# Spreading the conditioning vector on TensorE and summing the squares of x there as they land, in a transformer block on Trainium2

## Chip, cores and metric

One Trainium2 chip, one of its cores. The metric is the device time of one execution of the program, in microseconds (us), the median of several runs. Inputs come from the chip's HBM and outputs go back to it. The engines are TensorE (PE, its weight loads are PEld), VectorE (DVE), ScalarE (ACT), GpSimd (POOL) and SyncE (SP); SPq and ACTq are the instruction queues of an engine where they issue DMAs or wait.

## The reference

A block of three sublayers on x of 512 tokens by 1024 channels, in float32: a feed-forward layer, a hybrid mixer (pooling and a chunked state-space scan), and a second feed-forward layer, then a last normalisation. Each sublayer is modulated by a conditioning vector c of 1024 numbers:

```python
mod = (silu(c) @ w_ada + b_ada).reshape(1, 3, 3, 1024)
shift, scale, gate = mod[:, :, 0], mod[:, :, 1], mod[:, :, 2]
h = rmsnorm(x, norm_g[0]) * (1 + scale[:, 0]) + shift[:, 0]
x = x + 0.5 * gate[:, 0] * swiglu(h, ffn1_in, ffn1_out)
...
return rmsnorm(x, final_g)
```

The change touches only the way to the first h (the sum of squares of x over the 1024 channels of each token, its inverse root, and the first products of silu(c) with w_ada) and the very last stores.

## The kernel before

Activations lie transposed: 128 channels on the partitions, 512 tokens along the row, and 8 such tiles (k = 0 to 7) make x. All products run as three float32r passes (high times high, high times low, low times high) in `mm3` (L376 to L378), so every weight tile is split by ACT (the high part, L168) and DVE (the low part, L171). PE's instructions stand in the order in which the program writes them. In `first_pairs` (L742 to L864) this holds for all five engines, so whatever waits there holds up everything behind it on its engine.

**The start**, `first_pairs`. SP issues the loads in this order: four pairs of x tiles (L749, 512 KB each), c already copied to all 128 partitions on the host (L751, 512 KB), the small vectors `vec` (L752, 204 KB), then for k = 0 and 1 two rows of w_ada (L538: first the scale's, then the shift's, 512 KB each) and a block of first-layer weights (L126, 512 KB). A row buffer is one of two, so the rows of k = 2 are issued only when both rows of k = 0 have been used.

Meanwhile PE multiplies a tile of ones by itself (`warm`, L771), 24 products whose results nobody reads. A float32 product is two passes in the trace, each with a weight load of its own. ACT squares each pair of x tiles as it lands (L791, 1024 columns). DVE adds the first three pairs together (L793), folds the accumulated 1024 columns into 512, and folds the last pair the same way (L795). PE then sums over channels: `token_sums` (L490) is, for each chunk of 128 tokens, a product whose weights are the 128 by 128 chunk of squares and whose moving operand is one column of ones (L494). With two folded tiles and four chunks these are 8 products, 16 passes. ACT turns c into silu(c) (L797).

The DVE queue then holds, in this order: `ada_sum(1, 0)` (L549), which multiplies the scale's row of w_ada by silu(c) and adds it up; the inverse root on 128 by 4 numbers (L805, L806 and the nine operations of `inv_root`, L479 to L488); `ada_sum(0, 0)` for the shift; and L814, x times the spread root, called n0 below. Between the root and n0, PE spreads the root over the partitions (`spread`, L517). After the sums PE has 7 more products of ones (`WARM1`), after the spread 4 (`WARM2`).

From n0 ACT makes the high part of h[0] (L819), which releases the first product of weights (L847, 24 passes for k = 0, each 512 columns). For k = 1 to 7 `prepare` does two `ada_sum`s and L832 to L836, and PE runs 24 passes (L376 to L378) per k. Everything after is a long row of such products.

**The end**, `Final.finish` (L238 to L273). After the last product, PE transposes the second half of x (L249) and sums its squares (L494), DVE makes the root, and then two [128, 512] tiles are scaled by DVE (L270) and two by ACT (L268). Four stores of 256 KB (L273) all go out on SP's queue in the order DVE, ACT, DVE, ACT.

Of the kernel before, what the change touches and what calls it, by code (L numbers as in the profile page):

```python
# [11 lines left out]
AF = mybir.ActivationFunctionType  # L12
ALU = mybir.AluOpType
PSUM = bass.MemoryType.PSUM

P = 128
NT = 512
HT = 256
KD = 8
# [8 lines left out]
NCHK = 4  # L28
# [11 lines left out]
NBIG = 49  # L40
NSQ = 2
NTMP = 9
WARM = 24
WARM1 = 7
WARM2 = 4
BOOST = 2
SUMS_IN = 1
TURN = 7
# [181 lines left out]
class Final(Norm):  # L230
# [7 lines left out]
    def finish(self):  # L238
        blk, nc = self.blk, self.blk.nc
        chunks = range(HALF_B[0] // P, HALF_B[1] // P)  # L240
        n = len(chunks)
        banks = [[blk.bank() for _ in range(2)] for _ in chunks]
        todo = [(k, j) for k in range(KD) for j in range(n)]

        def turn(count):
            for k, j in todo[:count]:
                c = chunks[j]
                o = k % 4 * P
                nc.tensor.transpose(out=banks[j][k // 4][:, o:o + P], in_=blk.x[:, k, c * P:(c + 1) * P],  # L249
                                    identity=blk.ident)  # L250
            del todo[:count]

        turn(TURN)
        ps = blk.bank()
        for i, acc in enumerate(blk.accs[HALF_B]):
            blk.token_sums(ps, i * n, [acc], chunks)
        turn(len(todo))
        v, y, t, u = blk.root_tiles(n)
        count = KD * P
        V = nc.vector  # L260
        V.tensor_scalar(out=v, in0=ps[:, 0:n], scalar1=1.0 / count, scalar2=EPS, op0=ALU.mult, op1=ALU.add)
        V.scalar_tensor_tensor(out=v, in0=ps[:, n:2 * n], scalar=1.0 / count, in1=v, op0=ALU.mult, op1=ALU.add)
        blk.inv_root(v, y, t, u)
        stores = []
        for j, i in ((0, 0), (0, 1), (1, 0), (1, 1)):
            o = blk.big()
            if i:
                nc.scalar.activation(out=o, in_=banks[j][i], func=AF.Copy, scale=y[:, j:j + 1])  # L268
            else:
                V.tensor_scalar(out=o, in0=banks[j][i], scalar1=y[:, j:j + 1], scalar2=None, op0=ALU.mult)  # L270
            stores.append((blk.a["out1"][j * P:(j + 1) * P, i * NT:(i + 1) * NT], o))
        for dst, o in stores:
            nc.sync.dma_start(out=dst, in_=o)  # L273

    def apply(self, sl, k):
        blk = self.blk
# [6 lines left out]
class Block:  # L283
# [458 lines left out]
    def first_pairs(self):  # L742
        nc, sb, a = self.nc, self.sb, self.a
        V, S = nc.vector, nc.scalar
# [3 lines left out]
        for k in range(0, KD, 2):  # L748
            nc.sync.dma_start(out=self.x[:, k:k + 2, :], in_=a["x"][:, k:k + 2, :])  # L749
        self.cb = sb.tile([P, KD * P], F32, name="cb")  # L750
        nc.sync.dma_start(out=self.cb, in_=a["c"])  # L751
        nc.sync.dma_start(out=vec, in_=a["vec"])  # L752
        self.cst = cst
        self.vec = vec
# [4 lines left out]
        ones = sb.tile([P, P], F32, name="ones")  # L759
# [5 lines left out]
        t = self.tmp()  # L765
# [3 lines left out]
        def warm(n):  # L769
            for _ in range(n):  # L770
                nc.tensor.matmul(bank[:, 0:P], lhsT=ones, rhs=ones, start=True, stop=True)  # L771

        warm(WARM)
        rows = {}
# [9 lines left out]
        def row_tile():  # L784
            return self.W.pool.tile([P, KD * P], F32, name="w_hi", tag="w_hi", bufs=RING)

        psum = self.bank()
        acc, q = row_tile(), None
        for k in range(0, KD, 2):
            q = row_tile() if k else acc  # L790
            S.activation(out=q, in_=self.x[:, k:k + 2, :].rearrange("p k n -> p (k n)"), func=AF.Square)  # L791
            if k in (2, 4):
                V.tensor_tensor(out=acc, in0=acc, in1=q, op=ALU.add)  # L793
        for i, t in enumerate((acc, q)):
            V.tensor_tensor(out=t[:, :NT], in0=t[:, :NT], in1=t[:, NT:], op=ALU.add)  # L795
            self.token_sums(psum, i * NCHK, [(t, 0)], range(NCHK))
        S.activation(out=self.cb, in_=self.cb, func=AF.Silu)  # L797
        self.gb = sb.tile([P, 3, KD], F32, name="gb")
        self.hb = sb.tile([P, 3, KD], F32, name="hb")
        V.scalar_tensor_tensor(out=self.gb, in0=self.bada[:, 1::3, :], scalar=1.0, in1=self.ng,  # L800
                               op0=ALU.add, op1=ALU.mult)
        self.ada_sum(1, 0, rows[0][0])
        warm(WARM1)
        v, y, t, u = self.root_tiles(NCHK)
        V.tensor_scalar(out=v, in0=psum[:, 0:NCHK], scalar1=1.0 / (KD * P), scalar2=EPS, op0=ALU.mult, op1=ALU.add)  # L805
        V.scalar_tensor_tensor(out=v, in0=psum[:, NCHK:2 * NCHK], scalar=1.0 / (KD * P), in1=v,  # L806
                               op0=ALU.mult, op1=ALU.add)
        self.inv_root(v, y, t, u)
        rs = self.spread(y)
        warm(WARM2)  # L810
        h = self.new_h()
# [46 lines left out]
        a = self.a  # L858
# [364 lines left out]
def constants():  # L1223
    c = np.zeros((P, NCONST), np.float32)
    m, l = np.arange(P)[:, None], np.arange(P)[None, :]
    c[:, K_TRI:K_TRI + P] = m <= l
    at = K_CNT
    for win in (2, 4, 8, 16):
        c[:, at:at + win - 1] = win / np.arange(1, win, dtype=np.float32)
        at += win - 1  # L1230
    for h in range(NHEAD):
        c[[h, 32 + h, 64 + h, 96 + h], K_SEL + h] = 1.0
    return c


def arrange(inputs):

    v = {n: np.asarray(a) for n, a in inputs.items()}
    a = {}
    a["x"] = v["x"][0].T.reshape(KD, P, NT).transpose(1, 0, 2)  # L1240

    def cols(t):
        return t.reshape(-1, P).T

    a["c"] = np.tile(v["c"][0], (P, 1))
    vec = [cols(v["b_ada"][0]), cols(v["norm_g"][0].reshape(-1)), cols(v["final_g"]),
           v["conv_w"][0].reshape(4, 20, P).transpose(2, 1, 0).reshape(P, 80), cols(v["conv_b"][0]),
           cols(v["pool_scale"][0]), cols(v["ssm_norm_g"][0]), cols(np.repeat(v["d_skip"][0], 64)),
           np.tile(v["dt_bias"][0], (P, 1)), np.tile(v["a_log"][0], (P, 1)),
           np.eye(P, dtype=np.float32)]  # L1250
    a["vec"] = np.concatenate(vec, axis=1)
    assert a["vec"].shape == (P, NVEC)
    a["cst"] = constants()
    a["ada"] = v["w_ada"][0].T.reshape(9, KD, P, KD * P)

    def w_in(t):
        t = t[0].reshape(KD, P, 2, NPAIR, P)
        return t.transpose(3, 2, 1, 0, 4).reshape(2 * NPAIR, P, KD * P)

    def w_out(t, ks):  # L1260
        return t[0].reshape(-1, P, KD, P)[list(ks)].transpose(1, 2, 0, 3).reshape(P, -1)

    a["ffn1_in"] = w_in(v["ffn1_in"])
    a["w1s"] = a["ffn1_in"][:2 * FIRST[1]].reshape(2 * FIRST[1], P, KD, P).transpose(2, 1, 0, 3).reshape(KD, P, -1)
    a["ffn2_in"] = w_in(v["ffn2_in"])
    def w_quad(w, first):
        w = w.reshape(NPAIR, 2, P, 2, KD * P // 2)[first:]
        return np.stack([w[:, 1, :, 1], w[:, 0, :, 0], w[:, 1, :, 0], w[:, 0, :, 1]], axis=2).reshape(-1, P, 4 * NT)

    for f in (1, 2):  # L1270
        if QUADS[f] < NPAIR:
            a["ffn%d_inQ" % f] = w_quad(a["ffn%d_in" % f], QUADS[f])
        for i, (p0, p1) in enumerate(PORTIONS):
            a["ffn%d_out%d" % (f, i)] = w_out(v["ffn%d_out" % f], range(p0, p1))
    a["w_outA"] = w_out(v["w_out"], range(4, 10))
    a["w_outB"] = w_out(v["w_out"], LAST_KS)
    wi = v["w_in"][0]
    a["w_in"] = wi[:, :36 * P].reshape(KD, P, 36, P).transpose(2, 1, 0, 3).reshape(36, P, KD * P)
    a["w_inH"] = a["w_in"][4:8].reshape(4, P, 4, 2, P).transpose(2, 1, 3, 0, 4).reshape(4, P, KD * P)
    a["ffn2_inH"] = a["ffn2_in"][0:4].reshape(4, P, 4, 2, P).transpose(2, 1, 3, 0, 4).reshape(4, P, KD * P)  # L1280
    a["w_dt"] = np.zeros((P, KD, 32), np.float32)
    a["w_dt"][:, :, :NHEAD] = wi[:, 36 * P:].reshape(KD, P, NHEAD).transpose(1, 0, 2)
    a["w_dt"] = a["w_dt"].reshape(P, -1)
    a["w_pool"] = v["w_pool"][0].transpose(1, 0, 2).reshape(P, NT)
    return {n: np.ascontiguousarray(t) for n, t in a.items()}
# [18 lines left out]
```

## Time and profile before

| what | us |
|---|---|
| median of 3 runs | 1098.95 (1098.39 to 1099.58) |
| the profiled execution | 1098.18 |
| span from its first to its last instruction | 1096.3 |
| PE busy | 1075.5 |
| DVE busy | 851.2 |
| ACT busy | 500.6 |

Times in the trace are counted from the first instruction. The profiled execution takes 1.88 us beside its span and is 0.77 us under the median. A line of the timeline gives the start, the duration of the merged instructions, the engine, the line and operation, what it writes and reads, and in brackets how long the engine was idle before and what released it. For merged instructions the duration runs from the first start to the last end.

### The profile page before, as it was taken

What the parts mean: (1) busy time and instruction counts of PE and PEld (TensorE: products, weight loads), DVE (VectorE), ACT (ScalarE), POOL (GpSimd) and SP (SyncE); (2) the same over time, 40 slices, a digit from 0 to 9 for tenths busy, and PEclk for the clock granted to TensorE, in tenths of its full rate; (3) what the DMA queues carried; (4) which work ended last, traced back from release to release, by engine and by line L of the source; (5) the groups of instructions that cost most, each with busy time, mean ns of one, the idle gap of its engine ahead of it and who ended that gap; (6) DMA issues with size and microseconds to landing.
All of it is one profiled execution on the core that took longest, in us unless ns stands there. A gap on an engine that the chain in (4) does not pass through costs nothing.

```text
span 1096.3 us, 17024 instructions
## 1 busy us (share of the span) xinstructions
PE 1075.5 (98%) x6764; PEld 954.4 (87%) x6764; DVE 851.2 (78%) x1354; ACT 500.6 (46%) x836; POOL 116.9 (11%) x114
## 2 busy tenths in 40 slices
PE   8999999999999999999999999999999999999997
PEld 7888899999899988887888767899899999999997
DVE  7986978888887848989988777764877778777744
ACT  4442444454444544656565552354434434444532
POOL 0000000000001410012312850121000000000011
PEclk9999999999999999999999999999999999999999
DMA  8865334443346405554445335740132233223222
GB/s 326 305 225 175 127 120 135 144 144 126 111 158 204 152 25 167 173 168 138 144 135 182 122 120 173 231 153 20 42 113 86 91 113 107 95 87 101 75 58 78
DMA packets 45955, 149.43 MB, mean 136 GB/s; under 512 B 5276, under 2 KB 8220, under 8 KB 45876
## 3 DMA queue, kind: packets, MB, share of 16 engines
q1 hardware_dynamic: 45876, 148.35, 41.8%
q8 instruction: 53, 0.87, 0.3%
q14 instruction: 26, 0.21, 0.1%
HBM read 146.18 MB, written 2.15 MB: 135 GB/s over the span
## 4 chain that ended last, share of the span: by engine, by line
PE 72%; DVE 14%; DMA 7%; ACT 4%; issue 2%; POOL 1%; SPq 0%; DVEq 0%; ACTq 0%; POOLq 0%
PE ps_mm L377 19%; PE ps_mm L376 19%; PE ps_mm L378 18%; PE ps_t L376 4%; PE ps_t L377 4%; PE ps_t L378 4%; DVE w_lo L171 3%; DVE w_raw L549 2%; DMA w_raw<-in_w_in_dram 2%; ACT w_hi L168 2%; DVE big L969 2%; DMA w_raw<-in_ada_dram 1%; DMA big<-csd 1%; ACT big L1035 1%; DVE big L973 1%
## 5 line engine op out<-in xcount | busy, mean ns | idle before, releaser
L376 PE MATMUL ps_mm<-big,w_hi 128*128 128x512 f32 (+1 forms) x1446 | 494.3, 342 | 0.5 <-DVE tmp L452 0.5
L377 PE MATMUL ps_mm<-big,w_hi 128*128 128x512 f32 (+1 forms) x1446 | 492.5, 341 | 0.4 <-DVE big L836 0.4
L378 PE MATMUL ps_mm<-big,w_lo 128*128 128x512 f32 (+1 forms) x1446 | 490.9, 339 | 0.0
L376 PEld LDWEIGHTS ps_mm<-big,w_hi 128*128 128x128 f32 x1446 | 272.1, 188 | 35.3 <-issue 2.3
L377 PEld LDWEIGHTS ps_mm<-big,w_hi 128*128 128x128 f32 x1446 | 274.0, 190 | 32.2 <-DVE big L836 0.9
L378 PEld LDWEIGHTS ps_mm<-big,w_lo 128*128 128x128 f32 x1446 | 271.6, 188 | 30.8
L168 ACT CAST w_hi<-w_raw 128x1024 fp32r<-128x1024 f32 (+1 forms) x118 | 120.2, 1019 | 250.2 <-issue 92.0
L171 DVE TENSOR_TENSOR w_lo<-w_raw,w_hi 128x1024 fp32r<-128x1024 f32 (+1 forms) x118 | 143.9, 1221 | 43.8 <-ACT w_hi L168 40.8
L168 ACT CAST w_hi<-row 128x1024 fp32r<-128x1024 f32 x124 | 116.6, 940 | 89.3 <-PE ps_t L377 37.9
L171 DVE TENSOR_TENSOR w_lo<-row,w_hi 128x1024 fp32r<-128x1024 f32 x124 | 134.9, 1088 | 22.4 <-ACT w_hi L168 22.4
L603 DVE SCALAR_TENSOR_TENSOR x<-ps_mm,mod,x 128x512 f32<-128x512 f32 (+1 forms) x111 | 74.7, 675 | 78.5 <-PE ps_mm L378 78.5
L376 PE MATMUL ps_t<-big,w_hi 128*128 128x256 f32 (+1 forms) x428 | 126.8, 296 | 1.9 <-DVE tmp L440 1.7
L377 PE MATMUL ps_t<-big,w_hi 128*128 128x256 f32 (+1 forms) x428 | 127.0, 297 | 0.0
L378 PE MATMUL ps_t<-big,w_lo 128*128 128x256 f32 (+1 forms) x428 | 126.6, 296 | 0.0
L473 POOL TENSOR_TENSOR sacc<-sacc,sq 128x256 f32<-128x256 f32 (+1 forms) x30 | 28.5, 951 | 754.2 <-ACT sq L528 443.5
L376 PEld LDWEIGHTS ps_t<-big,w_hi 128*128 128x128 f32 x428 | 80.5, 188 | 6.6 <-DVE tmp L440 3.0
L377 PEld LDWEIGHTS ps_t<-big,w_hi 128*128 128x128 f32 x428 | 81.5, 191 | 3.6
L378 PEld LDWEIGHTS ps_t<-big,w_lo 128*128 128x128 f32 x428 | 80.4, 188 | 2.1
L467 ACT CAST big<-tmp 128x512 fp32r<-128x512 f32 (+1 forms) x82 | 44.1, 546 | 21.5 <-DVE tmp L400 9.6
L469 DVE TENSOR_TENSOR big<-tmp,big 128x512 fp32r<-128x512 f32 (+1 forms) x66 | 41.5, 640 | 8.0 <-ACT big L467 7.6
L969 DVE SCALAR_TENSOR_TENSOR big<-ps_mm,vec,big 128x511 f32<-128x511 f32 (+2 forms) x60 | 44.6, 744 | 1.5 <-ACT big L967 0.8
L135 DVE TENSOR_TENSOR row<-row 128x1024 f32<-128x1024 f32 x31 | 37.9, 1222 | 3.7 <-DMA row<-in_ffn_inQ_dram 3.1
(180 smaller groups left out, 1149.1 us busy)
## 6 DMA issues: line engine op xcount, KB each, us to landing
w_raw<-in_ada_dram SPq DMA_DIRECT2D x56, 512.0 KB, 3.7
row<-in_ffn_inQ_dram SPq DMA_DIRECT2D x31, 768.0 KB, 4.4
w_raw<-in_ffn_out_dram SPq DMA_DIRECT2D x40, 512.0 KB, 3.8
w_raw<-in_w_in_dram SPq DMA_DIRECT2D x32, 512.0 KB, 3.7
row<-in_ada_dram SPq DMA_DIRECT2D x16, 512.0 KB, 6.4
row<-in_ffn_inQ_dram SPq DMA_DIRECT2D x31, 256.0 KB, 4.7
w_raw<-in_ffn_in_dram SPq DMA_DIRECT2D x14, 512.0 KB, 4.5
big<-csd SPq DMA_DIRECT2D x24, 256.0 KB, 4.3
```

Of the source, the lines that this page charges most:

```text
L135: V.tensor_tensor(out=raw[:, 1:4:2], in0=raw[:, 0:3:2], in1=raw[:, 3:4].broadcast_to([P, 2, NT]), op=ALU.add)
L168: nc.scalar.copy(out=h, in_=r)
L171: nc.vector.tensor_tensor(out=l, in0=r, in1=h.bitcast(F32), op=ALU.subtract)
L376: T.matmul(o, lhsT=hi, rhs=ahi[:, s], start=first, stop=False, skip_group_check=again)
L377: T.matmul(o, lhsT=hi, rhs=alo[:, s], start=False, stop=False, skip_group_check=again)
L378: T.matmul(o, lhsT=lo, rhs=ahi[:, s], start=False, stop=last, skip_group_check=again)
L467: self.nc.scalar.copy(out=hi[:, s], in_=src[:, :n])
L469: eng.tensor_tensor(out=lo[:, s], in0=src[:, :n], in1=hi[:, s].bitcast(F32), op=ALU.subtract)
L473: self.nc.gpsimd.tensor_tensor(out=acc, in0=acc, in1=q, op=ALU.add)
L549: return self.nc.vector.tensor_tensor_reduce(out=w, in0=w, in1=self.cb, scale=scale, scalar=bias, op0=ALU.mult, op1=ALU.add, accum_out=out)
L603: self.nc.vector.scalar_tensor_tensor(out=xs, in0=ps[:, :n], scalar=self.mod[:, gate, m:m + 1], in1=xs, op0=ALU.mult, op1=ALU.add)
L969: V.scalar_tensor_tensor(out=acc[:, s:], in0=ps[:, :NT - s], scalar=tap(3 - s), in1=acc[:, s:], op0=ALU.mult, op1=ALU.add)
```

## The change

It is made in four places. c is loaded as one row of 4 KB by ACT's queue into partition 0 of `cb`, and PE spreads it over 128 partitions with two products of a row of ones by half of c (one weight row, 512 columns each); ACT applies silu from PSUM, half of c each time, behind its second and third square. The squares of each pair of x tiles are made half by ACT and half by DVE, and PE sums every one of the 8 tiles by `token_sums` as its pair comes, with no adding on DVE in between: 32 products instead of 8. One product of ones stands ahead of each but the first of these groups. The root, now of four partial sums, stands ahead of `ada_sum(1, 0)` on DVE. The products of ones are 10, 5 and 5 instead of 24, 7 and 4. Of the four last stores the second and the fourth go out on ACT's queue.

```diff
-WARM = 24
-WARM1 = 7
-WARM2 = 4
+WARM = 10
+WARM1 = 5
+WARM2 = 5
...
-        for dst, o in stores:
-            nc.sync.dma_start(out=dst, in_=o)
+        for n, (dst, o) in enumerate(stores):
+            (nc.scalar if n % 2 else nc.sync).dma_start(out=dst, in_=o)
...
-        nc.sync.dma_start(out=self.cb, in_=a["c"])
+        nc.scalar.dma_start(out=self.cb[0:1, :], in_=a["c"])
...
         psum = self.bank()
-        acc, q = row_tile(), None
-        for k in range(0, KD, 2):
-            q = row_tile() if k else acc
-            S.activation(out=q, in_=self.x[:, k:k + 2, :].rearrange("p k n -> p (k n)"), func=AF.Square)
-            if k in (2, 4):
-                V.tensor_tensor(out=acc, in0=acc, in1=q, op=ALU.add)
-        for i, t in enumerate((acc, q)):
-            V.tensor_tensor(out=t[:, :NT], in0=t[:, :NT], in1=t[:, NT:], op=ALU.add)
-            self.token_sums(psum, i * NCHK, [(t, 0)], range(NCHK))
-        S.activation(out=self.cb, in_=self.cb, func=AF.Silu)
+        cps = [self.bank() for _ in range(2)]
+        for i, k in enumerate(range(0, KD, 2)):
+            q = row_tile()
+            S.activation(out=q[:, :NT], in_=self.x[:, k, :], func=AF.Square)
+            V.tensor_tensor(out=q[:, NT:], in0=self.x[:, k + 1, :], in1=self.x[:, k + 1, :], op=ALU.mult)
+            if i == 0:
+                for j, ps in enumerate(cps):
+                    nc.tensor.matmul(ps, lhsT=ones[0:1, :], rhs=self.cb[0:1, j * NT:(j + 1) * NT], start=True, stop=True)
+            else:
+                warm(1)
+            self.token_sums(psum, i * NCHK, [(q[:, :NT], 0), (q[:, NT:], 0)], range(NCHK))
+            if i in (1, 2):
+                S.activation(out=self.cb[:, (i - 1) * NT:i * NT], in_=cps[i - 1], func=AF.Silu)
...
-        self.ada_sum(1, 0, rows[0][0])
         warm(WARM1)
         v, y, t, u = self.root_tiles(NCHK)
         V.tensor_scalar(out=v, in0=psum[:, 0:NCHK], scalar1=1.0 / (KD * P), scalar2=EPS, op0=ALU.mult, op1=ALU.add)
-        V.scalar_tensor_tensor(out=v, in0=psum[:, NCHK:2 * NCHK], scalar=1.0 / (KD * P), in1=v,
-                               op0=ALU.mult, op1=ALU.add)
+        for i in range(1, KD // 2):
+            V.scalar_tensor_tensor(out=v, in0=psum[:, i * NCHK:(i + 1) * NCHK], scalar=1.0 / (KD * P), in1=v,
+                                   op0=ALU.mult, op1=ALU.add)
         self.inv_root(v, y, t, u)
+        self.ada_sum(1, 0, rows[0][0])
         rs = self.spread(y)
...
-    a["c"] = np.tile(v["c"][0], (P, 1))
+    a["c"] = v["c"][0].reshape(1, KD * P)
```

## Rows read from the trace of the kernel before

**Rows 1.** The page, busy time of each engine over the span.

```profile
PE 1075.5 (98%) x6764; PEld 954.4 (87%) x6764; DVE 851.2 (78%) x1354; ACT 500.6 (46%) x836; POOL 116.9 (11%) x114
```

**Rows 2.** Windows: length, then PE, PEld, DVE, ACT, POOL busy, granted clock, DMA share, GB/s.

```profile
24.60:320.00 295.40, 293.46 (x1786) 260.99 (x1787) 249.92 (x361) 126.78 (x183) 0.00 (x0) 1.00 0.49 163
```

**Rows 3.** Waits of PE over the whole span: us in total, times, longest.

```profile
PE ps_mm L494 <- POOL big L473: 2.4, 1, 2.4
...
PE ps_mm L847 <- ACT big L819: 0.7, 1, 0.7
...
PE ps_mm L377 <- DVE big L836: 0.4, 1, 0.4
```

**Rows 4.** The chain that ended last, 0 to 60 us: start, duration, what.

```profile
11.81 1.34 DVE row L549
15.28 1.17 PE ps_mm L517 x8
```

**Rows 5.** The timeline of all engines, 0 to 24 us.

```profile
1.05 8.58 PE L771 MATMUL ps_mm<-ones 128*128 128x128 f32 x48 [1.05 <-DVE ones L760]
...
4.77 1.06 ACT L791 ACTIVATE w_hi<-x 128x1024 f32<-128x1024 f32 x1 [2.54 <-DMA x<-in_x_dram]
...
8.57 1.06 ACT L791 ACTIVATE w_hi<-x 128x1024 f32<-128x1024 f32 x1 [0.22 <-DMA x<-in_x_dram]
9.71 1.29 DVE L795 TENSOR_TENSOR w_hi<-w_hi 128x512 f32<-128x512 f32 x2
...
10.46 1.95 PE L494 MATMUL ps_mm<-ones,w_hi 128*128 128x1 f32 x16 [0.82 <-DVE w_hi L795]
...
11.81 1.34 DVE L549 CUSTOM_DVE_ANT_0 row<-row,cb,gb 128x1024 f32<-128x1024 f32 x1 [0.62 <-DMA row<-in_ada_dram]
...
13.08 0.16 DVE L805 TENSOR_SCALAR root<-ps_mm 128x4 f32<-128x4 f32 x1
...
15.06 0.16 DVE L488 SCALAR_TENSOR_TENSOR root<-root 128x4 f32<-128x4 f32 x1
15.14 1.28 DVE L549 CUSTOM_DVE_ANT_0 row<-row,cb,vec 128x1024 f32<-128x1024 f32 x1
...
16.47 0.69 DVE L814 TENSOR_TENSOR tmp<-x,ps_mm 128x512 f32<-128x512 f32 x1
...
17.91 0.56 ACT L820 COPY big<-ps_mm 128x512 f32<-128x512 f32 x1
...
18.06 2.13 PE L847 MATMUL ps_mm<-big,w_hi 128*128 128x512 f32 x8 [0.73 <-ACT big L819]
```

**Rows 6.** Line L751, the load of c on SP: issue in ns, and landing.

```profile
L751 SPq DMA_DIRECT2D cb<-in_c_dram x1: 656/656/656, 2.6 to 2.6; - x1
...
DMA to landing us min/median/max: 7.3/7.3/7.3
```

**Rows 7.** L771 passes from 1 to 7 and 7.5 to 9.6 us: ns, first and last start.

```profile
L771 PE MATMUL ps_mm<-ones x28: 421/421/579, 1.1 to 7.0; 128*128 128x128 f32 x28
...
L771 PE MATMUL ps_mm<-ones x20: 274/275/321, 7.2 to 9.4; 128*128 128x128 f32 x20
```

**Rows 8.** PE near 630 us: L888, float32 products of 512 columns: ns; timeline.

```profile
L888 PE MATMUL ps_t<-big x8: 592/592/697, 630.7 to 653.9; 128*128 128x512 f32 x8
...
630.75 1.98 PE L888 MATMUL ps_t<-big 128*128 128x512 f32 x4
```

**Rows 9.** L494 passes from 10 to 12.6 us: ns, first and last start.

```profile
L494 PE MATMUL ps_mm<-ones,w_hi x16: 250/250/271, 10.5 to 12.2; 128*128 128x1 f32 x16
```

**Rows 10.** Timeline of all engines from 1086 us to the end.

```profile
1090.61 1.41 DVE L270 TENSOR_SCALAR big<-ps_mm,root 128x512 f32<-128x512 f32 x2
1090.67 1.27 ACT L268 ACTIVATE big<-ps_mm,root 128x512 f32<-128x512 f32 x2 [2.38 <-DVE root L488]
1091.38 1.81 SPq L273 DMA_DIRECT2D out_dram<-big  x4
```

**Rows 11.** Windows of the last stores, columns as in rows 2.

```profile
1092.20:1094.80 2.60, 0.00 (x0) 0.00 (x0) 0.00 (x0) 0.00 (x0) 0.00 (x0) 0.60 1.03 399
```

## The prediction

> **What bounds the kernel now.** I read the page first: PE is busy for 98% of the span [rows 1]. The windows say the same of the long middle: from 24.6 to 320 us PE lacks 2 us of 295 [rows 2]. The waits of PE name no DMA anywhere; the longest is 2.4 us on POOL in the middle [rows 3], and the change does not touch it. So what comes after the first products is a row of PE work with no slack: if it starts later by some time, the end comes later by that time. The place to look is the start, and the release there is the wait for h[0] at L847 [rows 3].
>
> The chain of waits follows the start back: the scale's row of w_ada lands, `ada_sum(1, 0)` runs on DVE at 11.81, then the root, the spread on PE at 15.28, then n0 [rows 4]. The timeline gives the times of DVE: root from 13.08, its last operation at 15.06, `ada_sum(0, 0)` at 15.14, n0 at 16.47, and the first product of weights at 18.06 [rows 5]. The reader is to see two things. The sums of squares were done at 12.41 (10.46 and 1.95), 0.67 us before DVE came to the root, so they were not on the path. And the chain from n0 to 18.06 holds nothing that the change edits: **the first product comes 1.59 us after n0**, and the prediction is the move of n0.
>
> **c as one row.** It takes 512 KB and an issue of 0.66 us from SP's queue [rows 6]; the loads behind it (`vec`, rows, first weights) come about 1.3 us sooner, the step between the landings of x pairs of 512 KB, (8.57 - 4.77) / 3 [rows 5]. What that is worth depends on whether a row is still waited for; below it is not. The issue on ACT's queue stands ahead of ACT's table load; by SP's issues it costs 0.4 to 0.7 us [rows 6, 10], covered by the 2.54 us in which ACT waits for x [rows 5]. Without that cover the first square would be later by that much. When c lands is not in the trace: at best with the first x, as a bound from above 7.3 us after its issue, as the big load of c [rows 6]. I take it as there by 5.4, since 4 KB is less than a hundredth of a pair of x, and a pair landed at 4.77 in spite of 2 MB queued. The late end is a rival.
>
> **The first passes of PE.** Until about 7.3 us a pass of ones takes 421 ns and starts 0.219 us after the one before, (7.0 - 1.1) / 27; then 275 ns and 0.116, (9.4 - 7.2) / 19 [rows 7]. The window columns show a granted clock of 1.00 for both, so it is the durations that tell the lower level, 1.2 GHz, from 2.4, and PE had worked without a pause for 6.2 us when it rose. Ten products are 20 passes: 1.05 + 20 x 0.219 = 5.42, so the fourteen taken away do not leave PE idle. Then the spread of c, two products of 512 columns in 4 passes. The nearest row, 4 passes of the same form at full clock, gives (1.98 - 0.59) / 3 = 0.46 us each (0.59 is what one of those passes takes) [rows 8]; at the lower level twice that. If the clock rises at 7.3 as before, two passes are slow and two fast: 5.42 + 1.84 + 0.92 = **8.2**. Bounds: all four fast 7.3, all four slow 9.1.
>
> **The sums on PE.** Here is the cost. 8 tiles by 4 chunks are 32 products, 64 passes, where there were 16. A pass with one column still loads 128 by 128 weights, and 16 of them start every (12.2 - 10.5) / 15 = 0.113 us [rows 9], as long as a pass of 128 columns. So 64 take 7.25 us. One product of ones ahead of three of the groups is 6 x 0.116 = 0.70, the last pass ends 0.25 after its start [rows 9]: 8.2 + 7.25 + 0.70 + 0.25 = **16.4** against 12.41 before. A pair of x lands every 1.27 us and 16 passes take 1.81: PE falls behind the landings.
>
> The squares are hidden under this. A square of 512 columns lies between a copy of 512 (0.56) and half of two such adds on DVE (0.65) [rows 5]; ACT has four squares and two silus of that size, ready by about 9.6 as the last x lands at 8.57, and PE comes to the last group only near 14.3. If PE were fast the squares would bound it at 9.6. The saved DVE adds (L793, L795) are worth nothing for the same reason.
>
> **The root and the row sums on DVE.** DVE stands at the root until 16.4, and behind it in its queue are both `ada_sum`s and n0. The root has two more operations, 13 at 0.198 us (from 13.08 to 15.06 are ten steps); the next operation starts 0.08 after the last one's start. So `ada_sum(1, 0)` starts at 16.4 + 12 x 0.198 + 0.08 = 18.86. It takes 1.27 to the next start (11.81 to 13.08), `ada_sum(0, 0)` 1.33 (15.14 to 16.47) [rows 5]: n0 at **21.46**, against 16.47, or **+5.0 us**. The spread of the root (1.17 [rows 4]) lies beside the 2.6 us of row sums. Its WARM2 passes end before 21.2. The rows of w_ada, due before 11.8, and silu(c) are there long before 18.86, so the earlier landing buys nothing. The rows of k = 2 are issued after `ada_sum(0, 0)`, later by the same 5 us, and so are their users. Late next, once h[0] is there, is what was late before: L836 with 0.4 us [rows 3].
>
> **The stores.** DVE and ACT end their tiles at 1092.02 and 1091.94, and SP's four issues end at 1093.19 [rows 10]. With two on ACT behind its two tiles the last issue would end about 1092.8, 0.4 sooner. But from 1092.2 to 1094.8 the DMA engines run at 1.03 of their share, 399 GB/s, without a hole, for the 1 MB [rows 11], and the first store, which sets that start, stays where it was. I take 0; ends -0.4, and +0.1 for one more queue to be waited for.
>
> **Sum.** Profiled 1098.18 + 5.0 = 1103.2; the median stands 0.77 above that execution, so I say **1103.9**. From the bounds of the spread of c (7.3 to 9.1 in place of 8.2) and the stores: 1102.6 to 1104.9.
>
> **Rivals.**
> First, **the passes of the sums hide behind one another**, and it is not slower. For it: a weight load takes 0.19 and overlaps work already. Against it: 16 passes in a row whose squares were ready show 0.113 [rows 9]. It decides where n0 comes before 16.47, that is where the sums end before 16.47 - 2.60 - 2.46 = 11.4, at 0.035 us a pass. At 0.03 the last squares (9.6) bind: 9.6 + 0.48 + 0.25 + 2.46 + 2.60 = 15.4, so -1.1 us, 1097.9. This can't reach -0.2%. The Trainium skill, "TensorE: Matmul & The Clock Gate", section "Back-to-back issue gap", gives about 25 ns for passes of 1 to 64 columns, by which the 64 would take an estimated 1.6 us; the same section says that in a stream the weight loads count as well.
>
> Second, **the clock does not rise, or falls again, under passes of one column**. For it: in the trace it rose after 6.2 us of passes with 128 columns, and here 14 products of that kind go and thin ones come. Against it: it stayed up through a PE wait of 2.4 us [rows 3]. Passes at 0.219, as the slow ones of 128 columns [rows 7], add up to 64 x 0.106 = 6.8 us and the spread of c 0.9; the first weights could add some more: 1106 to 1112, as it lasts. The same page, in "Why this matters for your kernels", wants TensorE kept busy to get past the low clock and no gaps in it afterwards; whether passes of one column count as busy no run here shows.
>
> Third, **c lands late**, behind the x pairs at 8.6. PE idles from 5.4, the spread of c runs at the low level to 8.6 + 3.7 = 12.3, and n0 moves by 4.1 more: 1108.
>
> **Chances.** Forecast 0.70, passes hide (or something unseen makes up for the rest) 0.13, clock 0.10, c late 0.07. The range leaves out the first rival and the far part of the second: 1101.0 to 1109.0, the low end below the forecast's own 1102.6 in case part of the 5 us is made up later. 0.2% is 2.2 us, about what a measurement of this kernel can tell from no change: slower by more 0.87, within 0.09, faster 0.04 (only if the passes hide and the stores and the start gain more than I can find).
>
> **What would show it.** Right: L494 as 64 passes near 0.113 from about 8 to 16 us; L805 first in DVE's root with an idle of several us before it, released by PE L494; no wait of L549 for its row; L814 near 21.5 and L847 near 23; the last DMA traffic still 2.6 us long. Wrong: a root that starts before 12 us, or L771 and L517 passes of 421 ns after 8 us.

## The result, and the profile after

The changed kernel takes 1109.94 us (1108.12 to 1112.0, 4 runs) against 1099.26 (1098.39 to 1101.9, 4 runs): 1.0097 times as long, interval 1.0077 to 1.0116. Forecast were 1103.9 and slower; the sign is right, the size is twice what was forecast (10.7 us for 5.0) and lies above the range. The profiled execution takes 1109.12, its span is 1107.2 (1096.3 before).

The page shows PE busier than before, 1091.0 us for 1075.5 [rows 1], for the same result:

```profile
PE 1091.0 (99%) x6792; PEld 967.4 (87%) x6792; DVE 849.5 (77%) x1356; ACT 498.3 (45%) x837; POOL 117.1 (11%) x114
```

The timeline of the start (all engines, 0 to 32 us) answers to [rows 5]:

```profile
1.05 4.64 PE L771 MATMUL ps_mm<-ones 128*128 128x128 f32 x20 [1.05 <-DVE ones L760]
...
5.62 2.16 PE L795 MATMUL ps_mm<-cb,ones 1*128 1x512 f32 x4
...
7.71 2.03 PE L494 MATMUL ps_mm<-ones,w_hi 128*128 128x1 f32 x16
...
10.17 3.41 PE L494 MATMUL ps_mm<-ones,w_hi 128*128 128x1 f32 x16
...
14.01 3.41 PE L494 MATMUL ps_mm<-ones,w_hi 128*128 128x1 f32 x16
...
17.85 3.41 PE L494 MATMUL ps_mm<-ones,w_hi 128*128 128x1 f32 x16
...
21.30 0.16 DVE L807 TENSOR_SCALAR root<-ps_mm 128x4 f32<-128x4 f32 x1 [11.92 <-PE ps_mm L494]
...
23.84 1.34 DVE L549 CUSTOM_DVE_ANT_0 row<-row,cb,gb 128x1024 f32<-128x1024 f32 x1
...
26.32 0.68 DVE L818 TENSOR_TENSOR tmp<-x,ps_mm 128x512 f32<-128x512 f32 x1
...
27.90 2.13 PE L851 MATMUL ps_mm<-big,w_hi 128*128 128x512 f32 x8 [0.51 <-ACT big L823]
```

The reader is to see three things. The first group of 16 passes takes 2.03 us, the three later ones 3.41 each, though they are the same instructions. DVE stands 11.92 us at the root, with the row sum of 23.84 queued behind it, as forecast. And n0 (L818) comes at 26.32, 9.85 us later than before, the first product of weights at 27.90, 9.84 later: the loss is all there by then.

Why the groups differ is in the windows (length; PE, PEld, DVE, ACT, POOL busy; granted clock; DMA share; GB/s):

```profile
8.00:9.40 1.40, 1.40 (x14) 1.40 (x15) 0.87 (x3) 1.14 (x3) 0.00 (x0) 1.00 1.04 424
9.40:21.00 11.60, 11.60 (x57) 11.60 (x56) 0.00 (x0) 1.04 (x1) 0.00 (x0) 0.50 0.55 222
21.00:26.50 5.50, 5.21 (x24) 4.92 (x24) 4.79 (x18) 0.00 (x0) 0.00 (x0) 0.50 0.00 0
26.50:28.00 1.50, 0.99 (x9) 0.80 (x8) 1.50 (x2) 0.96 (x2) 0.00 (x0) 1.00 0.48 87
```

From 9.4 to 26.5 us the granted clock is 0.50, which is 1.2 GHz. Passes of one column start 0.113 us apart in the first group, (9.4 - 7.7) / 15, and 0.200 us apart in the second, (13.2 - 10.2) / 15:

```profile
L494 PE MATMUL ps_mm<-ones,w_hi x16: 250/250/337, 7.7 to 9.4; 128*128 128x1 f32 x16
...
L494 PE MATMUL ps_mm<-ones,w_hi x16: 212/352/352, 10.2 to 13.2; 128*128 128x1 f32 x16
```

Before it fell, PE had run the spread of c, with one weight row, and the first group of the sums. All the while the window gives PE as busy without a hole, 11.60 of 11.60. The Trainium skill, "TensorE: Matmul & The Clock Gate", section "Why this matters for your kernels", asks for a continuously busy TensorE with no long gaps; by that the clock should have stayed up. The trace differs: there was no gap, and it fell.

The stores moved nothing. The last traffic again runs without a hole, for about 2.6 us; this window of the changed kernel, 2.40 us of it, answers to [rows 11]:

```profile
1103.20:1105.60 2.40, 0.00 (x0) 0.00 (x0) 0.00 (x0) 0.23 (x1) 0.00 (x0) 0.50 1.06 408
```

From the first transposition (L249) to the end it is 9.7 us in both kernels.

From the first product of weights to that transposition it is 1068.5 us before and 1069.6 here. In the profiles of these two kernels and of the twelve below this stretch lies between 1066.4 and 1070.2, with no order by what was changed; so the 1.1 us beyond the 9.84 is within what the same work varies by.

### The profile page after: what moved, and what is told of

Its sections match the earlier page's. It is cut to its first block, busy times and chain, and to the rows that moved or that the text cites. A ratio compares the mean times of both kernels' runs of the same rounds, so it can differ in the third digit from the quotient of the medians.

```text
span 1107.2 us, 17084 instructions
## 1 busy us (share of the span) xinstructions
PE 1091.0 (99%) x6792; PEld 967.4 (87%) x6792; DVE 849.5 (77%) x1356; ACT 498.3 (45%) x837; POOL 117.1 (11%) x114
## 4 chain that ended last, share of the span: by engine, by line
PE 86%; DVE 7%; DMA 2%; ACT 2%; issue 1%; POOL 1%; ACTq 0%; SPq 0%; DVEq 0%; POOLq 0%
PE ps_mm L376 22%; PE ps_mm L377 22%; PE ps_mm L378 22%; PE ps_t L376 4%; PE ps_t L377 4%; PE ps_t L378 4%; PE ps_mm L494 2%; DVE w_lo L171 2%; DMA w_raw<-in_ada_dram 1%; DVE w_raw L549 1%; PE ps_y L1069 1%; ACT w_hi L168 1%; PE ps_y L1091 1%; PE ps_mm L771 1%; PE ps_t L1065 1%
```

## The experiments

Each ran beside the kernel before on its chip, and times are medians. Where a ratio is given it is to the kernel before, with its 95% interval. Two questions were asked: what made the clock fall, and how much of the 10.7 us each part of the change carries.

**1. Wide passes among the thin ones.** If passes of one column let the clock fall, passes of 128 columns among them might hold it.

```diff
-            self.token_sums(psum, i * NCHK, [(q[:, :NT], 0), (q[:, NT:], 0)], range(NCHK))
+            for j in range(NCHK):
+                self.token_sums(psum, i * NCHK + j, [(q[:, :NT], 0), (q[:, NT:], 0)], [j])
+                warm(1)
```

> The changed kernel with one more product of ones (128 columns) behind each two of the 32 products of the sums: 16 more products, 32 more passes of PE, nothing taken away. Theory (the clock fell because the sums are almost all passes of one column; passes of 128 columns among them hold it): every L494 pass starts 0.113 us after the one before as in the first group, no stretch of granted clock 0.5 between 9 and 26 us; a group takes 16 x 0.113 + 8 x 0.116 = 2.74 instead of 3.8, the root starts near 19.6 instead of 21.3 and x times the root near 24.6 instead of 26.3: about 1.7 us FASTER than the changed kernel in spite of the added work, 1108. Rival (the clock falls for another reason, such as the product with one weight row): passes stay at 0.200, the added ones cost 8 x 0.219 = 1.75 a group, the root starts near 26: 1114 or more. Rival (passes of the sums are slow by themselves when PE is fed in this order): 0.200 a pass at a granted clock of 1.00.

Measured: 1117.0 (1.0164, 1.0136 to 1.0193), 7 us slower than the changed kernel. In the profiled execution the clock did not even come up; L494, from 9 to 31 us:

```profile
L494 PE MATMUL ps_mm<-ones,w_hi x64: 212/352/373, 9.3 to 30.5; 128*128 128x1 f32 x64
```

and L771 in the same stretch:

```profile
L771 PE MATMUL ps_mm<-ones x37: 421/421/562, 10.2 to 30.7; 128*128 128x128 f32 x37
```

The 421 and 352 ns are those of the low level. The windows show a granted clock of 1.00 over all of it, as they do at the start of every kernel here while a pass of ones still takes 421 ns, so there it is the durations that must be read. The forecast time falls. But as the clock never came up in this execution, it can't tell whether the added passes would have held it. Two things were open: whether the added passes were too few, or the ten products ahead.

**2. The products of ones ahead, put back.** First alone, in the changed kernel, then together with experiment 1.

```diff
-WARM = 10
-WARM1 = 5
-WARM2 = 5
+WARM = 24
+WARM1 = 7
+WARM2 = 4
```

> The changed kernel with the products of ones of before (24, 7 and 4 instead of 10, 5 and 5); nothing else undone. Theory (products of ones bring the clock up, but the sums that follow let it fall again whatever went before): the clock is up by about 7 us, the ones end near 9.6, the spread of c runs at the full clock to 11.5, the first group of sums starts every 0.113 us, the later ones every 0.200, and the root starts near 25: 3 to 4 us SLOWER than the changed kernel, 1113. Rival (the fourteen products taken away are what lost the clock): no stretch at 0.5, sums at 0.113 to the end, root near 19.7: 1108 or less.

> The kernel with 16 more products of ones among the sums (e1) and 24 ahead instead of 10. Theory (in e1 the clock never came up because ten products end before it can; once up, passes of 128 columns among those of one column hold it): granted clock up by about 7 and no fall before the spread of the root, L494 passes 0.113 apart within a pair of products throughout, root near 23.4: 1110, some 7 us FASTER than e1 although 14 products more are made. This is then the price of the 64 passes at the full clock. Rival (passes of one column let the clock fall even so): 0.200 apart after the first group, root near 30: 1117 or more.

(The second has the edit of experiment 1, and of these three numbers it changes WARM alone.) Measured: 1112.83 (1.0126, 1.0113 to 1.0139) and 1116.0 (1.0154, 1.0138 to 1.017). The first is as expected: with the fourteen products put back it is 2.9 us slower than the changed kernel (the two intervals just overlap), and the clock falls all the same. Windows, up to its fall and from there:

```profile
1.00:11.70 10.70, 10.65 (x64) 9.28 (x65) 2.95 (x6) 4.86 (x8) 0.00 (x0) 1.00 0.94 356
11.70:28.00 16.30, 16.30 (x78) 16.30 (x78) 3.36 (x14) 1.05 (x2) 0.00 (x0) 0.50 0.25 102
```

The second is the rival's: the first group ran at the full clock, with its added passes, then it fell:

```profile
11.40:14.00 2.60, 2.60 (x24) 2.57 (x24) 0.00 (x0) 1.50 (x4) 0.00 (x0) 1.00 1.02 419
14.00:34.00 20.00, 20.00 (x94) 19.85 (x94) 2.96 (x14) 0.95 (x1) 0.00 (x0) 0.50 0.13 53
```

So it was not the ones ahead alone, and these added ones don't hold the clock here, where the spread of c stands ahead of them.

**3. The sums alone, in the kernel before**, with c from SP on 128 partitions and nothing else of the change, to see whether the spread of c is needed for the fall.

```diff
-            S.activation(out=q, in_=self.x[:, k:k + 2, :].rearrange("p k n -> p (k n)"), func=AF.Square)
...
+            S.activation(out=q[:, :NT], in_=self.x[:, k, :], func=AF.Square)
+            V.tensor_tensor(out=q[:, NT:], in0=self.x[:, k + 1, :], in1=self.x[:, k + 1, :], op=ALU.mult)
+            self.token_sums(psum, i * NCHK, [(q[:, :NT], 0), (q[:, NT:], 0)], range(NCHK))
```

> The kernel before with the squares summed on PE as they land and nothing else of the change: c on 128 partitions from SP, 24 products of ones, row sum ahead of the root, no single products of ones between the groups, stores on SP. Theory (the 64 passes are the loss, half by their number and half by the clock, and the spread of c with its one weight row is not needed for the fall): the clock falls among the sums, the root starts near 23 and x times the root near 27 instead of 16.47: 1109. Rival (the fall needs the spread of c): sums at 0.113, x times the root near 21.6: 1104.

Measured: 1105.53 (1.0059, 1.0041 to 1.0077), between the two. The mechanism is the theory's; the fall came later than it assumed, and n0 at 23.55 for 27. L494 ahead of it and behind it:

```profile
L494 PE MATMUL ps_mm<-ones,w_hi x37: 169/250/330, 8.9 to 12.8; 128*128 128x1 f32 x37
...
L494 PE MATMUL ps_mm<-ones,w_hi x28: 330/352/353, 12.8 to 18.5; 128*128 128x1 f32 x28
```

In this trace passes of one column are enough for the fall. But 36 of them ran at the full clock here, 16 in the changed kernel, where the spread of c stood ahead of them.

**4. Wider passes among the sums**, in the kernel of experiment 3, behind each two of the 32 products one of 512 columns.

```diff
-            self.token_sums(psum, i * NCHK, [(q[:, :NT], 0), (q[:, NT:], 0)], range(NCHK))
+            for j in range(NCHK):
+                self.token_sums(psum, i * NCHK + j, [(q[:, :NT], 0), (q[:, NT:], 0)], [j])
+                nc.tensor.matmul(bank, lhsT=ones, rhs=self.x[:, k, :], start=True, stop=True)
```

> The kernel e6 (before with the sums of squares on PE alone) with a product of 512 columns whose result nobody reads behind each two of the 32 products: 16 more, 32 more passes of 0.46. Theory (columns fed to PE hold the clock; in e7 the added 128 columns were too few): granted clock 1.00 from about 7 us to the first weights, L494 passes 0.113 apart in each pair of products to the end, so that the 64 passes alone cost 7.25 at the full clock; the root starts near 9 + 7.25 + 14.7 = 31. Rival (any stretch with passes of one column lets the clock fall): a stretch of 0.5, root near 45.

Measured: 1114.23, one run. The clock stayed, as expected; the window over the sums and L494 in it:

```profile
8.60:28.70 20.10, 20.10 (x97) 12.93 (x96) 2.00 (x6) 2.39 (x3) 0.00 (x0) 1.00 0.43 171
```

```profile
L494 PE MATMUL ps_mm<-ones,w_hi x64: 167/250/250, 8.6 to 28.4; 128*128 128x1 f32 x64
```

All 64 passes take 250 ns at most, where experiment 3, which lacks only the wide passes, has 352 from 12.8 us on. PE is busy without a hole in both; what differs is the work it is busy with. This is one trace of each. (The root started at 28.7, not 31: the passes cost less than I had allowed.)

**5. Rows instead of columns.** The spread of c has full columns but one weight row. Two kernels differ in that alone: the kernel before with the one row of c (17 products of ones ahead, seven behind the spread), and the same with the other 127 rows of c's tile set to zero and all 128 rows used. A third, without the seven, came first.

```diff
-        nc.sync.dma_start(out=self.cb, in_=a["c"])
+        nc.scalar.dma_start(out=self.cb[0:1, :], in_=a["c"])
...
+            nc.tensor.matmul(ps, lhsT=ones[0:1, :], rhs=self.cb[0:1, j * NT:(j + 1) * NT], start=True, stop=True)
...
+        warm(7)
```

and for the full rows

```diff
+        nc.gpsimd.memset(self.cb, 0.0)
...
-            nc.tensor.matmul(ps, lhsT=ones[0:1, :], rhs=self.cb[0:1, j * NT:(j + 1) * NT], start=True, stop=True)
+            nc.tensor.matmul(ps, lhsT=ones, rhs=self.cb[:, j * NT:(j + 1) * NT], start=True, stop=True)
```

> The kernel before with the one row of c, its load on ACT's queue and its spread on PE alone (17 products of ones ahead of it instead of 24, two silus from PSUM); sums, order on DVE and stores as before. Theory: the row of w_ada lands about 1.3 us sooner (near 10.4), ada_sum(1, 0) starts when DVE has folded, near 11.0 instead of 11.81, the root at the end of the sums near 12.45 instead of 13.08, x times the root near 15.85: 0.6 us FASTER than before, 1098.6. Rival (silu(c), now behind the last square, or the spread of c on PE binds the sums): same as before or up to 1 us slower.

> The kernel before with c as one row and its spread on PE (e4), and seven products of ones between the spread and the sums, where PE idled 2.6 us in e4 and the clock fell. Theory (e4 lost at the clock what the earlier row gave): clock 1.00 through the sums in most executions, x times the root near 15.9 to 16.5, and 0.5 to 1 us faster than e4: 1098.5, the same as before within what can be measured. Rival (the row of c is worth nothing for another reason): like e4, 1099.4.

> The kernel e8 (before with c as one row, filled with ones) with the other 127 partitions of c's tile set to zero by GpSimd and the spread made with all 128 weight rows instead of one: the same 4 passes of 512 columns and the same result. Theory (passes with one weight row count as little for the clock as passes of one column do): the clock does not fall behind the spread of c as it did in e8 at 9.8, the sums run at 0.113, x times the root near 16 instead of 17.9 in e8's trace: 1098.3, 1 us faster than e8 and perhaps 0.5 us faster than before. Rival (rows do not matter, the fall in e8 came from something else): a stretch of 0.5 behind the spread as in e8, 1099.3.

Measured: without the filling 1099.4 (1.0009, 0.9995 to 1.0023), so the 0.6 us that it was to gain did not come; filled 1099.31 (1.0007, 0.9996 to 1.0018), with full rows 1098.29 (0.9992, 0.9982 to 1.0002). By time none of these can be told from the kernel before. The traces can. With one row, the clock falls at the end of the spread, before any pass of one column, with ones of 128 columns on both sides:

```profile
7.50:9.70 2.20, 2.20 (x7) 0.95 (x7) 1.01 (x2) 1.12 (x2) 0.00 (x0) 0.97 1.01 380
9.80:13.00 3.20, 3.20 (x18) 3.20 (x16) 3.06 (x6) 1.86 (x3) 0.00 (x0) 0.50 1.03 422
```

With full rows it stays up through spread, sums and root:

```profile
6.50:8.20 1.70, 1.70 (x6) 0.75 (x5) 1.23 (x1) 0.59 (x2) 0.00 (x0) 1.00 0.98 344
8.20:18.00 9.80, 7.39 (x61) 6.82 (x59) 8.46 (x22) 4.57 (x7) 0.00 (x0) 1.00 0.89 339
```

That is one profiled execution of each. In the trace without the filling PE idles 2.59 us between the spread and the sums, and the clock falls as the sums begin (0.50 from 12 us). With full rows the earlier row of w_ada bought nothing even so: the last pair of x landed half a microsecond later (9.07 for 8.57), the row sum started at 11.80 for 11.81, and the first product of weights at 18.05 for 18.06.

**6. Full rows in the changed kernel.** The second edit of experiment 5, in the changed kernel.

> The changed kernel with the spread of c made with all 128 weight rows (the other 127 partitions of c's tile set to zero by GpSimd), everything else as changed. Theory (both thin kinds of pass count against the clock, but the 64 passes of one column are enough by themselves, as in e6): the clock comes up by the end of the spread in most executions, falls later among the sums than the 9.4 us of the changed kernel, after the second group rather than the first; the root starts near 19.5 instead of 21.3: 1108, 2 us faster than the changed kernel. Rival (the one weight row is what undoes the clock in the changed kernel): no stretch at 0.5, sums at 0.113 to the end, x times the root near 21.5 as first forecast: 1104. Rival (rows do not matter): like the changed kernel, 1110.

Measured: 1104.32 (1.0049, 1.0032 to 1.0065), 5.6 us faster than the changed kernel, and the first rival's number. That rival's mechanism isn't shown: the profiled execution was the slowest of four (1107.75, next to the theory's 1108), and there the clock fell at about 10.6 in spite of the full rows, with n0 at 25.80:

```profile
8.00:10.70 2.70, 2.70 (x25) 2.64 (x24) 1.51 (x4) 1.69 (x3) 0.00 (x0) 0.98 1.04 420
10.70:24.80 14.10, 13.82 (x66) 13.52 (x67) 3.59 (x16) 1.04 (x1) 0.00 (x0) 0.52 0.37 150
```

The other three (1103.51 to 1104.55) have mean clocks of 0.990 to 0.992, so they too had some low stretch; where, is open. By time, about half of the loss goes with the one row in this kernel. That it does so by way of the clock is argued from the two traces of experiment 5 and not shown here.

**7. Half the passes.** DVE adds the two squared tiles of each pair, so that PE makes 16 products and not 32.

```diff
-            self.token_sums(psum, i * NCHK, [(q[:, :NT], 0), (q[:, NT:], 0)], range(NCHK))
+            V.tensor_tensor(out=q[:, :NT], in0=q[:, :NT], in1=q[:, NT:], op=ALU.add)
+            self.token_sums(psum, i * NCHK, [(q[:, :NT], 0)], range(NCHK))
```

> The changed kernel with the two squared tiles of each pair added on DVE before the sums: 16 products, 32 passes, instead of 32 and 64; all else as changed. Theory (the passes of the sums set the root, half the passes half the loss, and at both levels of the clock): sums start near 7.7 as in the changed kernel, end near 14.3 with the clock falling among them, x times the root near 19.3, the first product of weights near 21 instead of 27.9: 1102.5, 7 us faster than the changed kernel. Rival (the loss sits in the order on DVE or in the spread of c, whatever the number of passes): 1108 or more.

Measured: 1101.2 (1.002, 1.0011 to 1.0029), 8.7 us faster than the changed kernel for the 7 of the theory. The clock fell here too, near 7.5, and n0 came at 19.51:

```profile
14.53 0.16 DVE L808 TENSOR_SCALAR root<-ps_mm 128x4 f32<-128x4 f32 x1 [3.34 <-PE ps_mm L494]
...
19.51 0.68 DVE L819 TENSOR_TENSOR tmp<-x,ps_mm 128x512 f32<-128x512 f32 x1
```

**8. The sums as before, the rest as changed**, with ten products of ones between the spread of c and the sums.

```diff
+        warm(10)
+        for k in range(0, KD, 2):
...
+            S.activation(out=q, in_=self.x[:, k:k + 2, :].rearrange("p k n -> p (k n)"), func=AF.Square)
+            if k in (2, 4):
+                V.tensor_tensor(out=acc, in0=acc, in1=q, op=ALU.add)
```

> The changed kernel with the sums as before (ACT squares each pair, DVE adds and folds, 8 products on PE), ten products of ones between the spread of c and the sums; the one row of c, the root ahead of the row sums and the two stores on ACT's queue stay. Theory (the 64 passes, at whatever clock, are the whole loss): sums end near 12.4, root 12.45 to 14.6, both row sums behind it, x times the root near 17.1 against 16.47 before and 26.3 in the changed kernel: 1100, 0.6 us above the kernel before, which is the price of the order on DVE, clock 1.00 through. Rival (the order on DVE, the spread of c or the stores carry a good part of the loss): 1102 or more.

Measured: 1099.75 (1.0011, 0.9997 to 1.0025). The time is the theory's, and the loss goes with the sums; of order, spread and stores together no more than 0.0025 is left. The one row of c stands in this kernel too, so the half of the loss that goes with it in experiment 6 goes with it only where the 64 passes stand behind it: the parts can't be added up. The trace is not what I expected. The clock was not up through all the ten (a pass takes 421 ns), it fell again behind the sums, and n0 came at 20.36 and not at 17.1:

```profile
9.32 4.64 PE L771 MATMUL ps_mm<-ones 128*128 128x128 f32 x20
13.75 1.96 PE L494 MATMUL ps_mm<-ones,w_hi 128*128 128x1 f32 x16
```

```profile
18.00:20.00 2.00, 2.00 (x9) 2.00 (x10) 2.00 (x3) 0.00 (x0) 0.00 (x0) 0.50 0.03 8
```

This execution took 1101.24, 1.5 us above the median; the others have no trace.

**9. The row sum ahead of the root**, in the changed kernel.

```diff
+        self.ada_sum(1, 0, rows[0][0])
         warm(WARM1)
...
-        self.ada_sum(1, 0, rows[0][0])
         rs = self.spread(y)
```

> The changed kernel with ada_sum(1, 0) ahead of the root on DVE, as before; all else as changed. Theory (DVE waits 11.9 us at the root with the row sum queued behind it, so the row sum put ahead costs nothing): x times the root comes 1.27 us sooner, near 25.0, and the time falls by 1.3 us, to 1108.7. Rival (the order is worth nothing because the spread of the root on PE at the low clock, 2.1 us, then binds, 23.7 + 2.1 = 25.8): 0.5 us.

Measured: 1107.8 (1.0089, 1.0057 to 1.0121), which by its interval can't be told from the changed kernel. The timeline of DVE says more:

```profile
10.75 1.34 DVE L549 CUSTOM_DVE_ANT_0 row<-row,cb,gb 128x1024 f32<-128x1024 f32 x1 [1.07 <-DMA row<-in_ada_dram]
21.37 0.16 DVE L808 TENSOR_SCALAR root<-ps_mm 128x4 f32<-128x4 f32 x1 [9.26 <-PE ps_mm L494]
...
23.82 1.28 DVE L549 CUSTOM_DVE_ANT_0 row<-row,cb,vec 128x1024 f32<-128x1024 f32 x1
26.06 0.69 DVE L818 TENSOR_TENSOR tmp<-x,ps_mm 128x512 f32<-128x512 f32 x1 [0.96 <-PE ps_mm L517]
```

The row sum now runs in the wait, but n0 moves from 26.32 to 26.06 only: it waits 0.96 us for the spread of the root, which takes 2.08 at the low clock (1.16 at the full one). The rival's mechanism is what the trace has.

## Why the prediction was right and wrong

**Right:** that the start sets the end. n0 moved by 9.85, the first product by 9.84, and what the rest added is within its own variation. That PE falls behind the landings, that DVE waits at the root with both row sums and n0 behind it (11.92 us), that no row of w_ada is waited for there, that the squares are hidden and the stores worth nothing. (The 0.4 us that an earlier last issue might have given was misread: of ACT's two issues one stands between its two tiles, not behind them, and ACT is idle for 0.46 us before the second tile.) The spread of c was up at 7.7 for 8.2, within its bounds. From the root's start to n0 it is 5.02 us (21.30 to 26.32), for 5.06.

**Wrong:** the step "64 passes at 0.113 us". The row [rows 9] was a right price for 16 passes behind 48 wide ones, and I carried it to 64 behind 20 wide ones and 4 with one weight row. Measured is 0.113 for the first group and 0.200 for the other three. The three products of ones between the groups went from 0.23 us each to about 0.6. The sums took 13.6 us for 8.2; they began 0.5 sooner than forecast and ended at 21.3 for 16.4. These 4.9 us are, to 0.1, the whole miss at n0 (26.32 for 21.46).

The second rival had named this, the clock that falls under passes of one column, and given 1106 to 1112. Its chance of 0.10 was the real mistake. What I held against it, that the clock stayed up through a PE wait of 2.4 us, says what a gap did and nothing of thin work. It also was a single execution: behind the same wait the clock falls in most of the other traces (last section). The trace of before has no stretch of more than 16 thin passes, so it could not speak against the rival. The chance should have been much larger, and the range should have reached up to the rival's 1112.

I had also priced the spread of c as 4 passes of a known length and not seen it as thin work. One trace of experiment 5 shows a fall behind it alone, and by the times of experiment 6 about half of the loss goes with its one row. In the changed kernel only the first of its four passes ran at the low level (871 ns, then 587), not two, which is why it was up early.

**The first rival** (passes that hide behind one another) is out: 0.113 and 0.200 throughout. **The third** is out too: the spread began 0.3 us behind the start of the last pass of ones, where one pass of ones follows another by 0.219, so it waited for c by about 0.1 us at most.

**Open:** the low level at the start ends at different times in executions of one kernel; in the changed kernel two of the four runs have mean clocks of 0.987 and 0.989 (1109.12, 1108.12) and two of 0.997 and 0.996 (1112.0, 1110.77). As the windows show 1.00 until the first change, the latter may never have come up, like the one of experiment 1; those runs have no trace.

## What to carry to other kernels

Moving additions to an idle TensorE as products with one column costs a full weight load for each 128 by 128 tile. Count these passes against what they replace: 64 passes did what two adds, two folds and 16 passes had done. Ask of each stretch of PE not only whether it is busy but with how many columns and rows. The clock fell here with PE busy throughout under long stretches of one column, and in one trace behind products of one row; until it came up again a pass of one column took 0.200 us for 0.113. A price taken from a short run of passes holds only with the clock that this run had.

## What was not expected of the hardware

The clock fell with PE busy 11.60 us of 11.60, which the column of busy time can't show; it stayed up in experiment 4 with passes of 512 columns among the 64, and not in experiment 2 with passes of 128. Experiment 2 also has the spread of c ahead of them, which experiment 4 has not, so the width alone isn't shown to make that difference.

It also falls once more in the middle. In the changed kernel PE waits 3.76 us for POOL at 630.8, and the granted clock is 0.50 behind it; before, the same wait is 2.37, and no window is below 1.00 there. The length of the wait alone doesn't decide it. The program there is the same in all the kernels. In eleven of the twelve traces of the experiments the clock falls in this wait or within 2.5 us of its end, also where it is 2.11 us long (experiment 4); in the one of experiment 7, with 2.18 us, it stays up. The filled kernel of experiment 5 falls with this wait, by its list of waits and its window:

```profile
PE ps_mm L494 <- POOL big L473: 2.2, 1, 2.2
...
620.00:630.00 10.00, 9.17 (x36) 8.10 (x37) 8.36 (x19) 3.21 (x6) 9.60 (x13) 0.66 0.20 73
```

So the trace of before, with the clock up all the way to the last stores, shows one execution and not what this stretch always does. PE's lines in the changed kernel there:

```profile
630.81 1.86 PE L494 MATMUL ps_mm<-ones,big 128*128 128x1 f32 x8 [3.76 <-POOL big L473]
...
642.97 1.05 PE L517 MATMUL ps_mm<-vec,root 128*128 128x128 f32 x8
```

Between these two lines lie 12.16 us, 9.01 before (619.06 to 628.07). The 3 us are made good within the next ten, at waits for DVE and ACT that the kernel before had and this one has no more, which is why they don't show in the sum.

The best of these kernels, with the one row of c spread by full rows and otherwise the sums, order and stores of before, is 0.9992 of the kernel before, 0.9982 to 1.0002: 1% faster than the changed kernel, not shown to be faster than the one before.
